# Two attention stages of a two-block transformer on one core: pairs of heads in steps with dense blocks between, and the softmax sum from a column of ones

## The chip, the cores and the metric

The kernel runs on one core of a Trainium2 chip. The metric is the device time of one execution in microseconds (us), as the median of several runs.

## What is computed

A block of 256 tokens by 1024 features runs through two models of two layers each: first gated linear attention with dense and expert feed-forward layers, then a second block whose layers are feed-forward, a mixer, an attention to a memory, and feed-forward, each with a residual and a layer norm. All of it is in fp32. The change touches the two mixers of the second block (stages `ab` and `mc`) and where the memory's keys and values are computed.

```
# ab: 8 heads of global attention and 8 heads in a window with a sink, 64 wide, 2 key heads each
s = q @ k.T * 64 ** -0.5;  p = softmax(s);  out_a = p @ v
s = where(|i - j| <= 128, s, -inf);  m = max(s.max(-1), sink)
p = exp(s - m);  p = p / (p.sum(-1) + exp(sink - m));  out_b = p @ v
y = concat(out_a, out_b) @ w_out
# mc: 16 heads of neighbourhood attention on a grid of 4 rows of 64, with a position bias
p = softmax(q @ k.T * 64 ** -0.5 + bias);  y = (p @ v) @ w_out
# memory attention, 4 heads of 256, behind each mixer
k, v = split(mem @ w_kv);  y = (softmax(q @ k.T / 16) @ v) @ w_o
```

## The kernel before

Weights are read from memory as tiles of 128 x 1024 (`split_weight`, L190): SP issues the load into `raw`, ScalarE rounds it to `whi` (L195), VectorE makes the rest `wlo` (L197). There are 7 buffers for `raw`, 9 for `whi` and 8 for `wlo`. Activations are kept as a high and a low part too (`xT`, `oT`), and a dense product is three matmuls per 128 rows of the contraction: high by high, low by high, high by low (`mm3`, L205, L207 to L209). `project` (L365) makes one or two blocks of 512 output columns of both halves `t` of the tokens, eight contraction steps each, so 24 matmuls of 512 columns for a block and half, and calls an epilogue. `out_ln` (L376) does the output projection over eight steps `k`, the residual, the layer norm and the transposition into `c.xT`.

The program is unrolled. A scheduler that knows what each instruction needs places the instructions of each engine in an order of its own, with the order of the text as priority. So work from further on in the text can stand between the pieces of a stage: the output projection of step `k` needs only the result of pair `k`.

In `mixer_ab` (L937) queries and keys of the first kind, values, and queries of the second kind come from three projected blocks (L1028, L1029). Then eight pairs of heads follow (`attend`, L1018). `mixer_c` (L1040) projects six blocks (L1097 to L1099), then has eight pairs (L1082). A pair (`pair_attention`, L920) does this:

- for each of its two heads: scores with the head's 64 features as contraction (L927), one accumulator bank for both halves of the tokens; then `soft_rows` (L870): the largest value of each row (L880 with a bias or a window, L888 without), exponentials on ScalarE with the sum of the row as a second output (L893), its reciprocal (L899), and a multiply of the probabilities by it (L901); then `rows_T` (L905): four transposes on TensorE (L911) and a copy out of PSUM, on ScalarE for the first head (L914) and VectorE for the second (L916).
- values (L932): the weights are the 64 columns of `v`, 256 columns of transposed probabilities move, the two heads write the two halves of the partitions. The result is already transposed and is split into `oT` (L285, L286), which is the same tile as `c.xT`.

The keys and values of the memory are made in eight blocks (`MemBlock`, L247): two tiles of the memory and four of weights are loaded, and two halves of dense work follow, each 24 matmuls of 512 columns or 48 of 256, each ending in a copy and a store to memory (L276, L277). `FILL` (L1153) says how many blocks go into which stage; the rest go to the start of the memory attention (L1113). Before, ab takes none and mc takes one. So mem0 has one and mem1 three.

Of the kernel before, what the change touches and what calls it, by code (L numbers as in the profile page):

```python
# [246 lines left out]
class MemBlock:  # L247
# [11 lines left out]

    def compute(self):  # L260
        c, nc = self.c, self.c.nc
        for half in range(2):
            ps = c.acc.tile([P, 512], F32, name="acc")
            if self.which == 0:
                for f in (2 * half, 2 * half + 1):
                    out = ps[:, 256 * (f % 2):256 * (f % 2) + 256]
                    for k in range(8):
                        wh, wl = self.us[k // 2]
                        sl = slice(512 * (k % 2) + P * f, 512 * (k % 2) + P * f + P)
                        mm3(c, out, wh[:, sl], wl[:, sl], *self.at(k, slice(0, 256)), k == 0, k == 7)  # L270
                o = 1024 * self.blk + 512 * half
            else:
                accumulate_k4(c, ps, lambda k: self.at(k, slice(half * P, half * P + P)), self.us)
                o = 1024 * half + 512 * self.blk
            s = c.tmp.tile([P, 512], F32, name="silu")
            nc.scalar.copy(s, ps)  # L276
            nc.sync.dma_start(c.kv[self.l][self.which][:, o:o + 512], s)  # L277
# [83 lines left out]
def tp_tile(c):  # L361
    return c.tp.tile([P, 512], F32, name="tp")

# [506 lines left out]
def soft_rows(c, ap, ps, mode, extra=None):  # L870
# [3 lines left out]
    sm = c.small.tile([P, 2], F32, name="ssm")  # L874
    p = ap.tile([P, 2, 256], F32, name="p", bufs=4)
    scale = [1.0, 1.0]
    if mode in ("bias", "window"):
# [8 lines left out]
        src = p  # L886
    else:
        nc.vector.tensor_reduce(nm, src, axis=AX.X, op=OP.max, negate=True)  # L888
        if extra is not None:
            nc.vector.tensor_mul(nm, nm, extra)  # L890
            scale = [extra[:, t:t + 1] for t in range(2)]
    for t in range(2):
        nc.scalar.activation(p[:, t], src[:, t], AF.Exp, bias=nm[:, t:t + 1], scale=scale[t],  # L893
                             accum_out=sm[:, t:t + 1])
    if mode == "window":
        es = c.small.tile([P, 2], F32, name="ses")
        nc.scalar.activation(es, nm, AF.Exp, bias=sink)
        nc.vector.tensor_add(sm, sm, es)
# [21 lines left out]
def pair_attention(c, ap, q, k, mode, extra, vsel, oT, k_out):  # L920
    nc = c.nc
    pT = []
    for a in range(2):
        r = slice(64 * a, 64 * a + 64)
        ps = acc_tile(c)
        for t in range(2):
            nc.tensor.matmul(ps[:, 256 * t:256 * t + 256], q[r, t * P:t * P + P], k[r], start=True, stop=True)  # L927
        pT.append(rows_T(c, ap, soft_rows(c, ap, ps, mode, extra(a)), a))
    po = tp_tile(c)
    for kb in range(2):  # L930
        for a in range(2):
            nc.tensor.matmul(po[64 * a:64 * a + 64, 0:256], vsel(a, kb), pT[a][:, kb], start=kb == 0, stop=kb == 1)  # L932
    split(c, po[:, 0:256], oT[0][:, k_out].rearrange("p t s -> p (t s)"),
          oT[1][:, k_out].rearrange("p t s -> p (t s)"))


def mixer_ab(c, X, xT, ln_idx):  # L937
    nc, A = c.nc, c.A
    with c.tc.tile_pool(name="ab", bufs=1) as ap:
        rope = ap.tile([P, 3, 2, 2, 64], F32, name="rope")  # L940
# [9 lines left out]
        v = ap.tile([P, 2, 256], F32, name="v")  # L950
# [30 lines left out]
        def k_epi(t, ps):  # L981
# [12 lines left out]
            nc.scalar.copy(v[:, t], ps[:, 256:])  # L994
# [16 lines left out]

        def epi0(t, pss):
            k_epi(t, pss[0])
            q_epi(t, pss[1], 0)

        oT = c.xT

        def attend(kind):  # L1018
            for hp in range(4):
                kv = hp // 2  # L1020
                pair_attention(
                    c, ap, qT[:, kind, hp], kT[:, kind, kv], "window" if kind else "plain",
                    (lambda a: ([win[:, 0], win[:, 1]], sink[:, 2 * hp + a:2 * hp + a + 1])) if kind else
                    (lambda a: rsq[:, :, 2 * hp + a]),
                    lambda a, kb: v[:, kb, 128 * kind + 64 * kv:128 * kind + 64 * kv + 64],
                    oT, 4 * kind + hp)
# [13 lines left out]
def mixer_c(c, X, xT, ln_idx):  # L1040
    nc, A = c.nc, c.A
    with c.tc.tile_pool(name="mc", bufs=1) as ap:
        nav = ap.tile([P, 64], F32, name="nav")
        nc.sync.dma_start(nav, A["nav"])
        rp = A["c_rpb"]
        v = ap.tile([P, 2, D], F32, name="v")
# [30 lines left out]
        def v_epi(t, ps, i):  # L1077
            nc.scalar.copy(v[:, t, 512 * i:512 * i + 512], ps)

        oT = c.xT  # L1080

        def attend(i):  # L1082
            for hq in range(4):
                hp = 4 * i + hq
                b = tb[hp // 2]
                if hp % 2 == 0 and hp > 0 and hp < 6:
                    tb.append(bias_tile(hp // 2 + 1))
# [13 lines left out]
        for b in extra:  # L1101
            b.load()
# [119 lines left out]
```

## Time and profile before

| | us |
|---|---|
| median of 3 runs | 2685.03 |
| lowest, highest | 2681.85, 2686.33 |
| profiled execution | 2683.43 |
| its span, first to last instruction | 2681.6 |
| TensorE busy (share of the span) | 2620.2 (98%) |
| VectorE busy | 1912.0 (71%) |
| ScalarE busy | 1492.6 (56%) |
| stage ab, attention alone | 1710 to 1766 of the span |
| stage mc, attention alone | 2302 to 2361 of the span |

The page of the profile gives for each engine its busy time, for forty slices of the span the busy tenths and the granted TensorE clock, and the costliest groups of instructions by line. Views of the trace give the same for any stretch, the waits of an engine with what ended them, and the instructions in order of time. A matmul's duration in these rows includes what it spends in the pipeline, so the distance from one start to the next says what it costs. One fp32 matmul shows as two records, one fp32 transpose as one.

### The profile page before, as it was taken

The page shows a single profiled execution, that of the slowest core. Times are in us where ns is not written, and L with a number is a line of the kernel's source. Part 1 is how long each engine was busy: PE and PEld are TensorE (multiplying, and loading weights), DVE is VectorE, ACT ScalarE, POOL GpSimd, SP SyncE. Part 2 cuts the span into 40 slices and gives each one's busy share as a digit, 9 for nine tenths or more (in the row PEclk, how much of TensorE's full clock was granted, in tenths as well). Part 3 has the DMA queues.
Part 4 walks back from the last instruction along what each step waited for, and adds up shares of the span by engine and source line. Part 5 has one row for each costly group of instructions (what it writes and reads, how often), then busy time and mean ns, then how long its engine had stood idle before and what let it go on. Part 6 is the DMA issues. An engine that isn't in the chain of part 4 may idle for free. (4 is left out here: it accounts for less than half of the span.)

```text
span 2681.6 us, 34175 instructions
## 1 busy us (share of the span) xinstructions
PE 2620.2 (98%) x12066; PEld 2103.9 (78%) x12066; DVE 1912.0 (71%) x2374; ACT 1492.6 (56%) x1844; POOL 46.9 (2%) x55
## 2 busy tenths in 40 slices
PE   8999999999999999999998999999999999999998
PEld 6888778877777877787776888678888888688887
DVE  6754668888888888888888555777546556575664
ACT  5444437677677677677666444544444444444452
POOL 1000000000000000000000000100000000000000
PEclk9999999999999999999999999899999999899999
DMA  7555537999999999999999654444555556445552
GB/s 291 174 184 177 205 118 281 340 354 341 340 346 344 347 338 353 347 338 338 361 335 339 220 188 157 168 159 163 183 194 204 188 194 194 131 173 220 204 199 91
DMA packets 193980, 658.64 MB, mean 246 GB/s; under 512 B 33094, under 2 KB 33288, under 8 KB 193288
## 3 DMA queue, kind: packets, MB, share of 16 engines
q1 hardware_dynamic: 193800, 656.37, 69.2%
q8 instruction: 96, 1.57, 0.2%
q14 instruction: 84, 0.69, 0.1%
HBM read 651.05 MB, written 5.24 MB: 245 GB/s over the span
## 5 line engine op out<-in xcount | busy, mean ns | idle before, releaser
L197 DVE TENSOR_TENSOR wlo<-raw,whi 128x1024 fp32r<-128x1024 f32 x1193 | 1407.3, 1219 | 244.7 <-ACT whi L195 114.3
L195 ACT CAST whi<-raw 128x1024 fp32r<-128x1024 f32 x1193 | 1194.0, 1051 | 373.6 <-PE acc L209 293.7
L207 PE MATMUL acc<-whi,xh 128*128 128x512 f32 x1376 | 546.0, 397 | 6.3 <-ACT whi L195 6.1
L209 PE MATMUL acc<-whi,xl 128*128 128x512 f32 x1376 | 539.4, 392 | 0.0
L208 PE MATMUL acc<-wlo,xh 128*128 128x512 f32 x1376 | 538.4, 391 | 0.1
L208 PE MATMUL acc<-wlo,xgh 128*128 128x512 f32 x896 | 356.6, 398 | 5.3 <-DVE wlo L197 5.3
L207 PE MATMUL acc<-whi,xgh 128*128 128x512 f32 x896 | 350.2, 391 | 1.8 <-ACT whi L195 1.8
L209 PE MATMUL acc<-whi,xgl 128*128 128x512 f32 x896 | 349.8, 390 | 0.0
L207 PEld LDWEIGHTS acc<-whi,xh 128*128 128x128 f32 x1376 | 259.2, 188 | 58.3 <-ACT whi L195 6.3
L209 PEld LDWEIGHTS acc<-whi,xl 128*128 128x128 f32 x1376 | 258.7, 188 | 55.4 <-issue 1.7
L208 PEld LDWEIGHTS acc<-wlo,xh 128*128 128x128 f32 x1376 | 259.3, 188 | 53.5 <-DVE wlo L197 1.6
L208 PEld LDWEIGHTS acc<-wlo,xgh 128*128 128x128 f32 x896 | 168.0, 188 | 63.1 <-DVE wlo L197 27.7
L207 PEld LDWEIGHTS acc<-whi,xgh 128*128 128x128 f32 x896 | 168.2, 188 | 40.8 <-ACT whi L195 4.8
L209 PEld LDWEIGHTS acc<-whi,xgl 128*128 128x128 f32 x896 | 168.3, 188 | 32.6
L208 PE MATMUL tp<-wlo,hTh 128*128 128x512 f32 x448 | 179.4, 400 | 7.1 <-DVE wlo L197 6.9
L209 PE MATMUL tp<-whi,hTl 128*128 128x512 f32 x448 | 177.6, 396 | 0.0
L207 PE MATMUL acc<-whi,hh 128*128 128x512 f32 x440 | 172.5, 392 | 0.0
L209 PE MATMUL acc<-whi,hl 128*128 128x512 f32 x440 | 171.3, 389 | 0.0
L208 PE MATMUL acc<-wlo,hh 128*128 128x512 f32 x440 | 171.3, 389 | 0.0
L207 PE MATMUL tp<-whi,hTh 128*128 128x512 f32 x448 | 153.3, 393 | 5.1 <-ACT whi L195 5.1
L285 ACT CAST xh<-tp 128x512 fp32r<-128x512 f32 (+1 forms) x68 | 36.1, 536 | 207.4 <-PE tp L294 158.2
L286 DVE TENSOR_TENSOR hl<-tp,hh 128x512 fp32r<-128x512 f32 (+1 forms) x60 | 38.8, 647 | 136.9 <-ACT hh L285 135.5
(241 smaller groups left out, 2423.8 us busy)
## 6 DMA issues: line engine op xcount, KB each, us to landing
raw<-moe_dram SPq DMA_DIRECT2D x672, 512.0 KB, 5.4
raw<-f_dram SPq DMA_DIRECT2D x330, 512.0 KB, 4.9
raw<-h_in_dram SPq DMA_DIRECT2D x40, 512.0 KB, 5.4
raw<-m_kv_dram SPq DMA_DIRECT2D x32, 512.0 KB, 5.0
raw<-c_in_dram SPq DMA_DIRECT2D x24, 512.0 KB, 5.2
raw<-h_out_dram SPq DMA_DIRECT2D x16, 512.0 KB, 4.5
raw<-memT_dram SPq DMA_DIRECT2D x16, 512.0 KB, 4.7
raw<-m_q_dram SPq DMA_DIRECT2D x16, 512.0 KB, 5.3
```

The source lines that it names most:

```text
L195: nc.scalar.copy(hi, raw)
L197: nc.vector.tensor_sub(lo, raw, hi.bitcast(F32))
L207: mm(ps, xh, wh, start=start, stop=False)
L208: mm(ps, xh, wl, start=False, stop=False)
L209: mm(ps, xl, wh, start=False, stop=stop)
L285: c.nc.scalar.copy(dh, ps)
L286: c.nc.vector.tensor_sub(dl, ps, dh.bitcast(F32))
```

## The change

Pairs become objects with four steps (`Pair`): `scores`, `turn` (transposes), `values`, `finish`. `attend` runs them overlapped: in step `i` first the dense fillers of that step, then `finish` of pair `i-1`, `turn` of pair `i`, `scores` of pair `i+1`, `values` of pair `i`. The fillers are the projections that only later pairs need (`late_steps`, one half of the tokens each) and the halves of the memory blocks (`MemBlock.steps`). In ab one filler goes with each of the eight pairs: two of the projection of the second kind's queries, six of three memory blocks. In mc ten: two, two, one, one for the second half's queries, keys and values, and one for each of the last four pairs, from two memory blocks. `FILL` changes from (2, (), 1, 0, 1) to (2, (), 1, 3, 2); mem0 and mem1 have none left.

The probabilities are no longer normalised. `v` has a 65th column of ones for each head (a `memset` on POOL); the values' product is turned round, so that transposed probabilities are the weights and the 65 columns move. The last column is the row sum. A reciprocal and one multiply out of PSUM normalise the 64 columns of both heads and halves; two transposes bring the result into the form of `oT`. `oT` is now a tile of its own in both stages. The filler tile `pad` shrinks from 48 to 32 columns. `soft_rows` stays as it was for the memory attention.

```diff
 class MemBlock:
+    def steps(self):
+        def first():
+            self.load()
+            self.half(0)
+
+        return [first, lambda: self.half(1)]
...
+def late_steps(c, xT, w, u0, epi):
+    us = []
+
+    def step(t):
+        if t == 0:
+            us.extend(units(c, w, u0, 2))
+        ps = acc_tile(c)
+        accumulate_k4(c, ps, tok(xT, t), us)
+        epi(t, ps)
+
+    return [lambda t=t: step(t) for t in range(2)]
...
-def pair_attention(c, ap, q, k, mode, extra, vsel, oT, k_out):
+class Pair:
+    def scores(self):
...
+            ex = self.extra(a)
+            p, src, nm, scale = row_max(c, self.ap, ps, self.mode, ex)
+            for t in range(2):
+                nc.scalar.activation(p[:, t], src[:, t], AF.Exp, bias=nm[:, t:t + 1], scale=scale[t])
+            if self.mode == "window":
+                self.es = self.es or c.small.tile([P, 2, 2], F32, name="ses")
+                nc.scalar.activation(self.es[:, :, a], nm, AF.Exp, bias=ex[1])
+            self.p.append(p)
+
+    def turn(self):
+        self.pT = [rows_T(self.c, self.ap, p, a) for a, p in enumerate(self.p)]
+
+    def values(self):
+        c, nc = self.c, self.c.nc
+        po = tp_tile(c)
+        pv = po[:, 0:260].rearrange("p (t a d) -> p t a d", t=2, a=2)
+        for a in range(2):
+            for t in range(2):
+                for kb in range(2):
+                    nc.tensor.matmul(pv[:, t, a, :], self.pT[a][:, kb, t * P:t * P + P], self.vsel(a, kb),
+                                     start=kb == 0, stop=kb == 1)
+        rc = c.small.tile([P, 2, 2], F32, name="src")
+        if self.es is None:
+            nc.vector.reciprocal(rc, pv[:, :, :, 64])
+        else:
+            nc.vector.tensor_add(rc, self.es, pv[:, :, :, 64])
+            nc.vector.reciprocal(rc, rc)
+        self.o = self.ap.tile([P, 2, 2, 64], F32, name="o", bufs=2)
+        nc.vector.tensor_mul(self.o, pv[:, :, :, 0:64], rc[:, :, :, None].to_broadcast([P, 2, 2, 64]))
+
+    def finish(self):
+        c = self.c
+        pt = tp_tile(c)
         for t in range(2):
-            nc.tensor.matmul(ps[:, 256 * t:256 * t + 256], q[r, t * P:t * P + P], k[r], start=True, stop=True)
-        pT.append(rows_T(c, ap, soft_rows(c, ap, ps, mode, extra(a)), a))
-    po = tp_tile(c)
-    for kb in range(2):
-        for a in range(2):
-            nc.tensor.matmul(po[64 * a:64 * a + 64, 0:256], vsel(a, kb), pT[a][:, kb], start=kb == 0, stop=kb == 1)
-    split(c, po[:, 0:256], oT[0][:, k_out].rearrange("p t s -> p (t s)"),
-          oT[1][:, k_out].rearrange("p t s -> p (t s)"))
+            c.nc.tensor.transpose(pt[:, t * P:t * P + P], self.o[:, t].rearrange("p a d -> p (a d)"), c.ident)
+        split(c, pt[:, 0:256], self.oT[0][:, self.k_out].rearrange("p t s -> p (t s)"),
+              self.oT[1][:, self.k_out].rearrange("p t s -> p (t s)"))
+
+
+def attend(pair, n, fillers):
+    cur, last = pair(0), None
+    cur.scores()
+    for i in range(n):
+        for f in fillers.get(i, ()):
+            f()
+        if last is not None:
+            last.finish()
+        cur.turn()
+        nxt = None
+        if i + 1 < n:
+            nxt = pair(i + 1)
+            nxt.scores()
+        cur.values()
+        cur, last = nxt, cur
+    last.finish()
...
 def mixer_ab(c, X, xT, ln_idx):
+        oT = pair_tile(ap, "oT")
...
-        oT = c.xT
...
         project(c, A["ab_in"], 0, 2, xT, epi0)
-        project(c, A["ab_in"], 4, 1, xT, lambda t, pss: q_epi(t, pss[0], 1))
-        extra = take(c, c.F[3])
-        for b in extra:
-            b.load()
-        attend(0)
-        attend(1)
-        for b in extra:
-            b.compute()
+        steps = late_steps(c, xT, A["ab_in"], 4, lambda t, ps: q_epi(t, ps, 1))
+        for b in take(c, c.F[3]):
+            steps += b.steps()
+        attend(pair, 8, {i: [f] for i, f in enumerate(steps)})
...
 def mixer_c(c, X, xT, ln_idx):
+        oT = pair_tile(ap, "oT")
...
         project(c, W, 0, 2, xT, lambda t, pss: (q_epi(t, pss[0], 0), k_epi(t, pss[1], 0)))
-        project(c, W, 4, 2, xT, lambda t, pss: (v_epi(t, pss[0], 0), q_epi(t, pss[1], 1)))
-        project(c, W, 8, 2, xT, lambda t, pss: (k_epi(t, pss[0], 1), v_epi(t, pss[1], 1)))
-        extra = take(c, c.F[4])
-        for b in extra:
-            b.load()
-        attend(0)
-        attend(1)
-        for b in extra:
-            b.compute()
+        project(c, W, 4, 1, xT, lambda t, pss: v_epi(t, pss[0], 0))
+        steps = []
+        for n, f in enumerate((q_epi, k_epi, v_epi)):
+            steps += late_steps(c, xT, W, 6 + 2 * n, lambda t, ps, f=f: f(t, ps, 1))
+        for b in take(c, c.F[4]):
+            steps += b.steps()
+        plan = {0: steps[0:2], 1: steps[2:4], 2: steps[4:5], 3: steps[5:6]}
+        for i, f in enumerate(steps[6:]):
+            plan.setdefault(4 + i % 4, []).append(f)
+        attend(pair, 8, plan)
...
-FILL = (2, (), 1, 0, 1)
+FILL = (2, (), 1, 3, 2)
```

## Rows read from the trace of the kernel before

**Rows 1.** The page, forty slices of the span: granted TensorE clock in tenths.

```profile
PEclk9999999999999999999999999899999999899999
```

**Rows 2.** Windows over the attentions: length, busy us (instructions) per engine, clock, DMA share, GB/s.

```profile
1710.25:1765.60 55.35, 52.19 (x223) 28.40 (x221) 34.33 (x133) 29.04 (x91) 0.00 (x0) 0.88 0.09 29
2302.10:2361.00 58.90, 55.50 (x232) 33.72 (x232) 35.44 (x146) 26.92 (x84) 0.00 (x0) 0.74 0.28 63
```

**Rows 3.** Windows cut where the granted clock changes, ab first, then mc.

```profile
1716.60:1730.20 13.60, 12.82 (x32) 6.31 (x32) 6.32 (x22) 5.74 (x19) 0.00 (x0) 0.50 0.00 0
1730.20:1765.60 35.40, 35.29 (x170) 19.55 (x169) 23.40 (x102) 19.91 (x67) 0.00 (x0) 1.00 0.00 1
2307.10:2317.30 10.20, 10.18 (x29) 5.62 (x29) 4.94 (x25) 3.01 (x12) 0.00 (x0) 0.50 0.58 91
2317.30:2331.00 13.70, 12.07 (x59) 6.64 (x60) 10.24 (x40) 6.64 (x21) 0.00 (x0) 1.00 0.41 59
2331.00:2351.50 20.50, 19.87 (x62) 11.85 (x60) 11.89 (x53) 8.15 (x28) 0.00 (x0) 0.50 0.00 0
2351.50:2361.00 9.50, 9.50 (x64) 6.65 (x62) 5.05 (x18) 4.14 (x13) 0.00 (x0) 1.00 0.01 2
```

**Rows 4.** Waits of TensorE in the two attentions: us in total, times, longest.

```profile
PE acc L927 <- ACT p L893: 2.5, 1, 2.5
...
PE tp L911 <- DVE p L901: 1.8, 2, 1.1
```

**Rows 5.** Timeline of TensorE's matmuls in ab at full clock: start, length, group.

```profile
1753.77 0.65 PE L932 MATMUL tp<-pT,v 128*64 128x256 f32 x2
1754.35 0.50 PE L207 MATMUL acc<-whi,xh 128*128 128x512 f32 x1
1754.69 0.39 PE L208 MATMUL acc<-wlo,xh 128*128 128x512 f32 x1
1755.01 1.08 PE L932 MATMUL tp<-pT,v 128*64 128x256 f32 x6
1756.02 0.50 PE L209 MATMUL acc<-whi,xl 128*128 128x512 f32 x1
...
1756.58 0.60 PE L911 MATMUL tp<-cst,p 128*128 128x128 f32 x4
1756.94 0.48 PE L208 MATMUL acc<-wlo,xh 128*128 128x512 f32 x1
...
1757.96 0.39 PE L209 MATMUL acc<-whi,xl 128*128 128x512 f32 x1
1758.18 0.39 PE L207 MATMUL acc<-whi,xh 128*128 128x512 f32 x1
```

**Rows 6.** Timeline of TensorE in the first stage, fp32 products with few moving columns.

```profile
30.89 0.95 PE L466 MATMUL tp<-cst,m 128*128 128x2 f32 x8
31.70 0.49 PE L208 MATMUL acc<-wlo,xh 128*128 128x512 f32 x1
...
65.80 1.13 PE L580 MATMUL tp<-vg,wsm 128*128 128x128 f32 x8 [1.20 <-DVE vg L576]
66.69 0.48 PE L207 MATMUL acc<-whi,xh 128*128 128x512 f32 x1
```

**Rows 7.** Groups by line, ab's attention, then its full-clock stretch: busy us, mean ns, idle.

```profile
L901 DVE TENSOR_SCALAR p<-p,ssm 128x256 f32<-128x256 f32 x32 | 9.9, 347 | 0.0
...
L911 PE MATMUL tp<-cst,p 128*128 128x128 f32 x53 | 10.1, 290 | 0.1
L207 PE MATMUL acc<-whi,xh 128*128 128x512 f32 x9 | 3.9, 428 | 0.0
```

**Rows 8.** The page, costliest groups: the VectorE half of splitting a weight tile.

```profile
L197 DVE TENSOR_TENSOR wlo<-raw,whi 128x1024 fp32r<-128x1024 f32 x1193 | 1407.3, 1219 | 244.7 <-ACT whi L195 114.3
```

**Rows 9.** Windows, columns as in rows 2: ab's start, and mc's end with mem1.

```profile
1673.90:1684.90 11.00, 11.00 (x53) 8.94 (x52) 11.00 (x17) 4.91 (x7) 4.41 (x7) 1.00 0.86 299
2361.00:2470.00 109.00, 108.94 (x577) 92.76 (x576) 72.80 (x91) 56.49 (x79) 1.83 (x2) 1.00 0.67 241
```

More of the change, by code (lines that the diff above doesn't have):

```diff
@@ L258, in at, with half @@
         return [x[:, o + sl.start:o + sl.stop] for x in self.m[k // 4]]
+    def half(self, half):
+        c, nc = self.c, self.c.nc
+        ps = c.acc.tile([P, 512], F32, name="acc")
+        if self.which == 0:
+            for f in (2 * half, 2 * half + 1):
+                out = ps[:, 256 * (f % 2):256 * (f % 2) + 256]
+                for k in range(8):
+                    wh, wl = self.us[k // 2]
+                    sl = slice(512 * (k % 2) + P * f, 512 * (k % 2) + P * f + P)
+                    mm3(c, out, wh[:, sl], wl[:, sl], *self.at(k, slice(0, 256)), k == 0, k == 7)
+            o = 1024 * self.blk + 512 * half
+        else:
+            accumulate_k4(c, ps, lambda k: self.at(k, slice(half * P, half * P + P)), self.us)
+            o = 1024 * half + 512 * self.blk
+        s = c.tmp.tile([P, 512], F32, name="silu")
+        nc.scalar.copy(s, ps)
+        nc.sync.dma_start(c.kv[self.l][self.which][:, o:o + 512], s)
     def compute(self):
-        c, nc = self.c, self.c.nc
         for half in range(2):
[L263 to L277, printed above, removed]
+            self.half(half)
+    def steps(self):
[3 more added lines that the diff above has]
+        return [first, lambda: self.half(1)]
 def take(c, n):
@@ L867, in crowded, with row_max @@
             step()
[L870 removed]
+def row_max(c, ap, ps, mode, extra):
     nc = c.nc
@@ L885, in soft_rows @@
             nc.vector.tensor_scalar(nm, nm, sink, -1.0, op0=OP.max, op1=OP.mult)
[L886 to L891, printed above, removed]
-    for t in range(2):
[L893 to L898, printed above, removed]
+        return p, p, nm, [1.0, 1.0]
+    nc.vector.tensor_reduce(nm, src, axis=AX.X, op=OP.max, negate=True)
+    if extra is None:
+        return p, src, nm, [1.0, 1.0]
+    nc.vector.tensor_mul(nm, nm, extra)
+    return p, src, nm, [extra[:, t:t + 1] for t in range(2)]
+def soft_rows(c, ap, ps):
+    nc = c.nc
+    sm = c.small.tile([P, 2], F32, name="ssm")
+    p, src, nm, _ = row_max(c, ap, ps, "plain", None)
+    for t in range(2):
+        nc.scalar.activation(p[:, t], src[:, t], AF.Exp, bias=nm[:, t:t + 1], accum_out=sm[:, t:t + 1])
     nc.vector.reciprocal(sm, sm)
@@ L949, in mixer_ab @@
         qT = ap.tile([P, 2, 4, 256], F32, name="qT")
-        v = ap.tile([P, 2, 256], F32, name="v")
+        v = ap.tile([P, 2, 4, 65], F32, name="v")
+        nc.gpsimd.memset(v[:, :, :, 64:65], 1.0)
         tab = ap.tile([P, 2, 2, 2, 64], F32, name="tab")
@@ L1010, in q_epi, with pair @@
             nc.scalar.copy(qT[:, kind, :, t * P:t * P + P], pt.rearrange("p (b s) -> p b s", b=4))
+        def pair(i):
+            kind, hp = i // 4, i % 4
+            kv = hp // 2
+            return Pair(
+                c, ap, qT[:, kind, hp], kT[:, kind, kv], "window" if kind else "plain",
+                (lambda a: ([win[:, 0], win[:, 1]], sink[:, 2 * hp + a:2 * hp + a + 1])) if kind else
+                (lambda a: rsq[:, :, 2 * hp + a]),
+                lambda a, kb: v[:, kb, 2 * kind + kv], oT, i)
         def epi0(t, pss):
@@ L1045, in mixer_c @@
         rp = A["c_rpb"]
-        v = ap.tile([P, 2, D], F32, name="v")
+        v = ap.tile([P, 2, 16, 65], F32, name="v")
+        nc.gpsimd.memset(v[:, :, :, 64:65], 1.0)
         qT = [ap.tile([P, 4, 256], F32, name=f"qT{i}") for i in range(2)]
@@ L1077, in v_epi @@
         def v_epi(t, ps, i):
[L1078 to L1087, printed above, removed]
-                pair_attention(
-                    c, ap, qT[i][:, hq], kT[i][:, hq], "bias",
-                    lambda a: ([b[:, 2 * (hp % 2) + a, 2 * t:2 * t + 4, :].rearrange("p u c -> p (u c)")[:, ::-1]
-                                for t in range(2)], None),
-                    lambda a, kb: v[:, kb, 128 * hp + 64 * a:128 * hp + 64 * a + 64],
-                    oT, hp)
+            nc.scalar.copy(v[:, t, 8 * i:8 * i + 8, 0:64], ps.rearrange("p (h d) -> p h d", d=64))
@@ L1170, in body @@
         xT = c.xT = pair_tile(c.xtp, "x")
-        nc.gpsimd.memset(pad.tile([P, 48], F32, name="pad"), 0.0)
+        nc.gpsimd.memset(pad.tile([P, 32], F32, name="pad"), 0.0)
         c.early = []
```

43 lines of the change are left out of this document (25 added, 18 removed).

## Prediction

> **What bounds the kernel now.** I went from the whole to the stage. The page's line of the granted TensorE clock [rows 1] is full in nearly every fortieth of the span; its two dips, the 26th and the 35th slice (67 us each), are the two stages that the diff touches. TensorE is busy almost throughout, so in this kernel a microsecond counts when TensorE stands still, runs at half clock, or gets more work. The other engines matter only through these three.
>
> Next the windows over the two attentions [rows 2]: 55.35 us in ab and 58.90 us in mc, with mean clocks 0.88 and 0.74. Busy time there is 52.19 and 55.50 us, but busy says little, since a matmul at half clock counts as busy for twice as long. Cutting the windows where the clock changes shows it [rows 3]. In ab 13.6 us are at 0.50 (1.2 GHz) and 35.4 us at 1.00 (2.4 GHz). In mc 10.2 and 20.5 us are at 0.50, 13.7 and 9.5 us at 1.00. Before the fall in ab TensorE stood still for 2.5 us on the first exponentials (L893), and one of its waits in mc is on the normalisation L901, which this change removes [rows 4]. The full-clock stretch of ab matters for later: the same attention, with only some 25 dense matmuls strewn into it (9 of them the L207 of a triple), kept 2.4 GHz for 35 us [rows 3, 7]. DMA moved next to nothing there and VectorE was busy 34.33 of 55.35 us, so neither bounds [rows 2].
>
> **Step 1, half clock.** The dense work that used to come before and after the attention (late projections, memory blocks) now stands between the pairs: 8 half-blocks of 24 matmuls with 512 columns in ab (or 48 with 256), 10 in mc, one or two per pair. TensorE then has something to run while a softmax is under way. I price it by records per us. In ab 32 records took 13.6 us at half clock, and 170 took 35.4 us at full clock, 0.208 us each; 32 x 0.208 = 6.7, so 6.9 us go. In mc 29 + 62 = 91 records took 30.7 us, and 59 + 64 = 123 took 23.2 us at full clock, 0.189 each; 91 x 0.189 = 17.2, so 13.5 us go. **Together -20.4 us.** Most of the expected gain is here.
>
> **Step 2, standing still.** Idle TensorE is 55.35 - 52.19 = 3.2 us in ab and 58.90 - 55.50 = 3.4 us in mc [rows 2]; of that 0.8 and 0.6 us lie in the half-clock stretches and are already counted [rows 3]. The rest, 2.4 + 2.8, should be covered by the dense halves: **-5.2 us**. If the cover is not ready in time this term is zero.
>
> **Step 3, values.** Before, a pair's value product is 8 records with 256 moving columns on two column halves of the array. In two runs of the timeline they take 1754.35 - 1753.77 = 0.58 and 1756.02 - 1755.01 = 1.01 us, 1.59 together [rows 5]. After, it is 16 records: the probabilities are the 128x128 weights, 65 columns move (64 values and the column of ones), and each fp32 product is two records, as now. No row has 65 columns, so I bound it by rows with the same weights: 2 columns, eight in 31.70 - 30.89 = 0.81 us; 128 columns, eight in 66.69 - 65.80 = 0.89 us [rows 6]. Both ends are close, so the weight load sets it: 16 records take 1.62 to 1.78 us. I take the upper. The result lies by query rows now, so `finish` adds two transposes; four cost 1756.94 - 1756.58 = 0.36 [rows 5], two 0.18, plus some 0.07 to get in and out. Sum per pair 1.78 + 0.25 - 1.59 = 0.44 us (0.21 at the low end), sixteen pairs: **+7.0 us** (+3.4). This is real work on the busiest engine, and the price of the new form.
>
> **Step 4, dense matmuls in a row.** A dense 512-column matmul in a block starts 0.22 us after the one before (1757.96 to 1758.18), a lone one between attention pieces 0.34 (1754.35 to 1754.69) [rows 5]. In ab some dozen of the 25 in the full-clock stretch pay that 0.1 us; in mc I assume the same. Blocks of 24 don't: **-2 us**, with 0 and -3 as ends, because whoever orders the queue may still cut the blocks.
>
> **Step 5, VectorE and ScalarE.** Gone are the normalisation L901, 9.9 us in one attention [rows 7], and the read of the row sum behind each exponential on ScalarE. Added per pair are a small reciprocal, one multiply of 256 columns out of PSUM and, in window mode, one small add; the nearest row for the multiply is L901's 347 ns, its upper bound twice that, at most 16 x 1 us with the rest. TensorE doesn't feel either: **0 us**, hidden under some 10 us per pair of TensorE work. Without the cover the longer end of a pair (multiply, transposes, split) would cost about 1.5 us once per stage, behind the last pair.
>
> **Step 6, what moves.** The memory blocks leave mem0 (one) and mem1 (three) for ab (three) and mc (two, one of them there before). Their TensorE time is the same in either place, since mem1 with the end of mc is busy 108.94 of 109.00 us [rows 9]: 0 us. Without them the projection behind `out_ln` must cover the layer norm alone. The start of ab has just that form: 11.00 of 11.00 us busy, at full clock, with VectorE busy for all 11.00 too [rows 9], so it holds but has no slack. Each block brings six weight tiles, at 1219 ns of VectorE each [rows 8], 7.3 us for two pair steps of some 10 us; VectorE was 60% busy and loses L901, so it fits. On SP each `kv` store waits for its half-block's copy, and the weight loads queued behind it wait too; then `split_weight` is late for the next half-block. As DMA share was 0.09 in ab [rows 2], I cost it at nothing, with the ends in the next step. The `memset` of the ones on POOL and the smaller pad cost nothing. `oT` in its own tile lets late projections still read `xT`; by itself it gives no time.
>
> **Step 7, new waits.** Six tiles for a half-block that is due after some 5 us of attention may come late, the half-clock stretches may not all go, and the last pair's chain stands bare. From zero to 8 us (half of the 16 pairs late by 1 us, the size of one tile); I take **+3**.
>
> **Sum.** -20.4 - 5.2 + 7.0 - 2 + 3 = -17.6 us. The profiled execution took 2683.43 us (span 2681.6); so 2665.8. The median of the three runs, 2685.03, lies 1.6 above it, so I forecast 2667.
>
> **A rule against it.** In ab's full-clock stretch 53 transposes are among the 170 records, and the clock is 1.00 throughout [rows 3, 7]. The Trainium skill ("TensorE: Matmul & The Clock Gate", Part 4: PE-mode transpose) states that transposes don't count as activity for the clock in the way that matmuls do. The change adds transposes and takes moving columns away, so by that rule the clock would fall between the blocks (rival C). The trace doesn't bear it out so far.
>
> **Rivals.** *A, the forecast*, 0.63: -17.6. Its own range runs from all ends favourable (+3.4, -3, 0: -25) to all unfavourable (+7, 0, +8: -10.6): 2660 to 2674.
> *B, half of it stays*, 0.17: blocks are drawn ahead of the pairs that should be covered, and half of the half-clock time remains: +10.2, 2677. Still faster.
> *D, the blocks wait for weights*, 0.10: six tiles take 7.3 us on VectorE, the attention piece beside them has about 3.3 us of its own VectorE work ((34.33 - 9.9) / 8 = 3.05, and some of late epilogues), against 5 us of TensorE attention; 3 us late at each of five blocks, or about 15 us in all: 2682, no measurable change. For it: VectorE without slack in the 11.00 us window [rows 9]. Against: those are 10 us steps, not 5.
> *C, the clock falls between the dense blocks*, 0.10, the other side: the attention pieces are now narrower (65 columns) and follow each other in 5 us pieces, 16 x 5 = 80 us of them (records of step 3, plus scores and transposes at 0.2 us). Each us at 1.2 GHz costs half a us. From 47 us of half clock on it is slower by 5.4 us; at 55 us it is 2667 + 27 = 2694. Against it stand the 35.4 us at 1.00 with far less dense work [rows 3].
> That the order isn't as the text has it, is in B.
>
> **How the numbers follow.** A difference of 0.2% (5.4 us) is about what a measurement of this kernel can tell from no change. A and B are faster, 0.80; D is the same, 0.10; C is slower, 0.10. The range reaches from 2655 (A's best end with a little more of the standing still) to 2684, which takes in B and D and leaves C out and a little below.
>
> **What would show it.** Step 1: mean clock of ab and mc attention near 1.00, no stretch at 0.50 over 7 us. Step 2: no wait of TensorE over 1 us there. Step 3: the value records some 0.11 us apart, 16 to a pair. Step 4: dense matmuls 0.23 us apart in runs of twenty or more. Step 6: mem0 and mem1 each shorter by their blocks' time, busy as before. Wrong if TensorE waits for ScalarE's or VectorE's weight tiles inside the attention (D), or if half clock appears between blocks (C).

## The result and the profile after

The changed kernel takes 2656.42 us (median of four runs, 2655.05 to 2656.5) against 2685.42 for the kernel before in the same comparison: a ratio of 0.9893, interval [0.9876, 0.991]. That is 29.0 us less. The prediction had 2667 in a range of 2655 to 2684: the direction and the wide range hold, the latter by 1.4 us at its low end. The forecast's own range ended at 2660: its sum had left out a term of 10 us, the scores, and had a smaller one with the wrong sign.

The page after, to be held against [rows 1]: its first line, TensorE's busy time, and the clock in forty slices.

```profile
span 2654.6 us, 34354 instructions
...
PE 2596.9 (98%) x12226; PEld 2110.3 (79%) x12226; DVE 1899.9 (72%) x2306; ACT 1483.8 (56%) x1780; POOL 46.8 (2%) x57
...
PEclk9999999999999999999999999999999999999999
```

The two dips of the kernel before are gone. The windows over the two attentions (ab from the first scores to the last pair, then mc; columns as in [rows 2]) say it more sharply:

```profile
1701.20:1781.20 80.00, 78.73 (x543) 68.08 (x544) 52.85 (x120) 45.52 (x82) 1.63 (x1) 1.00 0.45 149
2281.20:2370.70 89.50, 88.87 (x503) 72.44 (x502) 57.70 (x136) 51.83 (x83) 0.00 (x0) 1.00 0.61 185
```

They are longer than the 55.35 and 58.90 us of [rows 2] because dense work has moved in, and the clock is 1.00 (2.4 GHz) in both, where it was 0.88 and 0.74. TensorE stands still for 1.27 and 0.63 us, where it was 3.2 and 3.4. All its waits in ab, then in mc (us in total, times, longest), against [rows 4]:

```profile
PE acc L955 <- ACT kT L1077: 0.8, 1, 0.8
PE acc L955 <- DVE ry L1056: 0.5, 1, 0.5
PE tp L975 <- ACT pT L936: 0.3, 2, 0.2
```

```profile
PE tp L1141 <- ACT qs L1136: 0.3, 1, 0.3
PE tp L1141 <- DVE qs L1138: 0.2, 1, 0.2
```

None is on an exponential, a normalisation or a weight tile.

Where the time goes by stage can be read from POOL. The last layer-norm instruction of each stage is the second of its pair at L328 (`lrs`). In the timeline of POOL (start, length, group) the last one ahead of ab, of ab, of mem0, ahead of mc, of mc and of mem1:

```profile
1681.67 0.92 POOL L328 TENSOR_TENSOR lrs<-lrs,cst 128x1 f32<-128x1 f32 x1 [5.05 <-DVE lrs L327]
...
1813.68 0.93 POOL L328 TENSOR_TENSOR lrs<-lrs,cst 128x1 f32<-128x1 f32 x1 [14.31 <-DVE lrs L327]
...
1877.82 0.92 POOL L328 TENSOR_TENSOR lrs<-lrs,cst 128x1 f32<-128x1 f32 x1 [14.32 <-DVE lrs L327]
```

```profile
2251.23 0.92 POOL L328 TENSOR_TENSOR lrs<-lrs,cst 128x1 f32<-128x1 f32 x1 [5.02 <-DVE lrs L327]
...
2402.92 0.92 POOL L328 TENSOR_TENSOR lrs<-lrs,cst 128x1 f32<-128x1 f32 x1 [14.32 <-DVE lrs L327]
...
2467.03 0.92 POOL L328 TENSOR_TENSOR lrs<-lrs,cst 128x1 f32<-128x1 f32 x1 [14.32 <-DVE lrs L327]
```

So ab takes 1813.68 - 1681.67 = 132.0 us, mem0 64.1, mc 151.7 and mem1 64.1, together 411.9. The same marks in the trace of before give 109.3, 75.0, 159.4 and 97.3, together 441.0. The difference is 29.1 us. The two profiled executions differ by 27.0 (spans of 2681.6 and 2654.6), because everything outside these four stages takes 2240.6 us in the one and 2242.7 in the other; of the ten kernels in the table below seven lie from the one to the other, these two among them, so the gain is in the four stages. mem0 and mem1 are shorter by 10.9 and 33.2 us, one and three blocks of 10.9 to 11.1; ab takes in three blocks for 22.7 more, and mc takes in one block and is still 7.7 shorter.

One group of the timeline of TensorE explains a part of this that the prediction had left out. A pair in ab, after:

```profile
1731.53 0.38 PE L990 MATMUL tp<-cst,o 128*128 128x128 f32 x2
1731.75 1.04 PE L933 MATMUL tp<-cst,p 128*128 128x128 f32 x8
1732.71 1.14 PE L955 MATMUL acc<-kT,qT 64*128 64x256 f32 x8
1733.78 2.00 PE L975 MATMUL tp<-v,pT 128*128 128x65 f32 x16
1735.59 0.48 PE L207 MATMUL acc<-whi 128*128 128x512 f32 x1
...
1740.93 0.39 PE L209 MATMUL acc<-whi,wlo 128*128 128x512 f32 x1
1741.16 0.38 PE L990 MATMUL tp<-cst,o 128*128 128x128 f32 x2
```

The second line of score matmuls, L955: eight records, four for each head, from 1732.71 to the next start at 1733.78, which is 1.07 us. Experiment 5 shows what four of them cost alone.

### The profile page after: what moved, and what is told of

Same layout as the page of the kernel before. It is cut to its first block, busy times and chain, and to the rows that moved or that the text cites. A ratio compares the mean times of both kernels' runs of the same rounds, so it can differ in the third digit from the quotient of the medians.

```text
span 2654.6 us, 34354 instructions
## 1 busy us (share of the span) xinstructions
PE 2596.9 (98%) x12226; PEld 2110.3 (79%) x12226; DVE 1899.9 (72%) x2306; ACT 1483.8 (56%) x1780; POOL 46.8 (2%) x57
## 5 line engine op out<-in xcount | busy, mean ns | idle before, releaser
L207 PE MATMUL acc<-whi,xh 128*128 128x512 f32 x1312 | 522.0, 398 | 6.6 <-ACT whi L195 6.3
L209 PE MATMUL acc<-whi,xl 128*128 128x512 f32 x1312 | 514.9, 393 | 0.0
L208 PE MATMUL acc<-wlo,xh 128*128 128x512 f32 x1312 | 514.1, 392 | 0.0
L207 PEld LDWEIGHTS acc<-whi,xh 128*128 128x128 f32 x1312 | 247.5, 189 | 56.5 <-ACT whi L195 6.3
L209 PEld LDWEIGHTS acc<-whi,xl 128*128 128x128 f32 x1312 | 247.0, 188 | 52.0 <-issue 0.5
L208 PEld LDWEIGHTS acc<-wlo,xh 128*128 128x128 f32 x1312 | 247.5, 189 | 50.1 <-DVE wlo L197 0.8
L295 ACT CAST xh<-tp 128x512 fp32r<-128x512 f32 x52 | 30.2, 588 | 172.9 <-PE tp L304 159.2
```

The costliest lines, as they stand in the source:

```text
L207: mm(ps, xh, wh, start=start, stop=False)
L208: mm(ps, xh, wl, start=False, stop=False)
L209: mm(ps, xl, wh, start=False, stop=stop)
L295: c.nc.scalar.copy(dh, ps)
```

## The experiments

Every kernel here computes the whole result. The experiments carry the numbers of their kernels. The theories that the expectations name are these.
- Theory 1: dense blocks between the pairs give the gain, since TensorE no longer falls to half clock. Rival 2: the new pair form (steps, column of ones) gives it, wherever the dense work stands.
- Rival 3 is about the scores: it says that it is worth nothing whether the two heads' scores stand next to each other on TensorE.
- Theory 4: the overlapped steps keep TensorE fed. Theory 5: the column of ones does, by taking the normalisation out of the chain from scores to transposes.
- Theories 6 to 8 are told with their runs.

All times by run, with the ratio to the kernel before in the same comparison and its interval; then the stages by the marks above, and the time at half clock inside the attentions of ab and mc. The kernel before was measured anew with each group of experiments, at 2682.57 to 2685.42 us, so a difference of 2 or 3 us between two rows of different groups tells nothing.

| kernel | us | ratio | ab | mem0 | mc | mem1 | half clock, ab / mc |
|---|---|---|---|---|---|---|---|
| before | 2685.42 | 1 | 109.3 | 75.0 | 159.4 | 97.3 | 13.7 / 30.7 |
| after | 2656.42 | 0.9893 [0.9876, 0.991] | 132.0 | 64.1 | 151.7 | 64.1 | 0 / 0 |
| e1 old places of dense work | 2670.75 | 0.9954 [0.9938, 0.9969] | 108.3 | 75.0 | 145.7 | 97.3 | 13.7 / 0 |
| e2 old values, dense blocks | 2649.66 | 0.9874 [0.9859, 0.9889] | 126.3 | 64.1 | 146.7 | 64.1 | 0 / 0 |
| e3 no memory blocks moved | 2661.41 | 0.9918 [0.9903, 0.9934] | 102.5 | 75.0 | 142.2 | 97.4 | 0 / 0 |
| e5 heads' scores apart | 2666.48 | 0.9936 [0.9922, 0.995] | 137.4 | 64.1 | 157.4 | 64.1 | 0 / 0 |
| e7 steps alone | 2699.04 | 1.0059 [1.0042, 1.0076] | 113.0 | 75.0 | 167.0 | 97.3 | 23.9 / 47.8 |
| e8 dense blocks alone | 2657.64 | 0.9906 [0.9889, 0.9922] | 131.9 | 64.1 | 153.8 | 64.1 | 0 / 0 |
| e9 old places, ones, and normalised | 2711.4 | 1.0105 [1.0088, 1.0122] | 114.9 | 75.1 | 174.6 | 97.3 | 23.9 / 58.0 |
| e10 old places, old order, ones | 2671.84 | 0.9958 [0.9941, 0.9974] | 108.7 | 75.0 | 146.1 | 97.4 | 13.7 / 0 |

**1. The dense work back at its old places.** The new steps and the column of ones stay; the late projections and memory blocks stand before and after the attention again, and `FILL` is the old one.

```diff
-        steps = late_steps(c, xT, A["ab_in"], 4, lambda t, ps: q_epi(t, ps, 1))
-        for b in take(c, c.F[3]):
-            steps += b.steps()
-        attend(pair, 8, {i: [f] for i, f in enumerate(steps)})
+        project(c, A["ab_in"], 4, 1, xT, lambda t, pss: q_epi(t, pss[0], 1))
+        extra = take(c, c.F[3])
+        for b in extra:
+            b.load()
+        attend(pair, 8, {})
+        for b in extra:
+            b.compute()
...
-FILL = (2, (), 1, 3, 2)
+FILL = (2, (), 1, 0, 1)
```

> The new pairs (column of ones, overlapped steps, own oT) with the dense work where it stood before: projections ahead of the attention, memory blocks as before. Theory 1 (the dense blocks between the pairs give the gain: they keep 2.4 GHz, fill the waits, and leave both heads' scores side by side): the half clock and the waits return and the new value form costs its 7 us, so 2680 to 2692 us, with stretches at clock 0.50 in both attentions. Rival 2 (the new form of the pair gives it: no normalisation on the way from exponential to transposes, steps overlapped): within 6 us of the changed kernel, 2652 to 2662 us, no half clock.

Measured: 2670.75 us, between the two ranges. The windows show why neither number fits. ab, cut where its clock changes, then the whole attention of mc:

```profile
1711.80:1717.60 5.80, 3.86 (x22) 2.67 (x21) 4.45 (x9) 3.07 (x4) 0.00 (x0) 1.00 0.75 258
1717.60:1731.30 13.70, 13.12 (x46) 9.06 (x48) 5.21 (x13) 7.06 (x15) 0.00 (x0) 0.50 0.00 1
1731.30:1766.80 35.50, 34.55 (x240) 28.23 (x240) 20.81 (x76) 16.70 (x42) 0.00 (x0) 1.00 0.00 1
2302.40:2347.00 44.60, 42.63 (x306) 35.29 (x306) 29.29 (x114) 23.94 (x51) 0.00 (x0) 1.00 0.35 79
```

ab falls for 13.7 us as before, mc not at all. So for the full clock the dense blocks are needed in ab, while something in the pair's new form is enough in mc. Theory 1 holds for one stage of two.

**2. The value product as it was, with the steps and the dense blocks of the change.** Probabilities are normalised again ahead of the transposes.

```diff
+            nc.vector.reciprocal(sm, sm)
+            for t in range(2):
+                nc.vector.tensor_scalar(p[:, t], p[:, t], sm[:, t:t + 1], None, op0=OP.mult)
...
-                    nc.tensor.matmul(pv[:, t, a, :], self.pT[a][:, kb, t * P:t * P + P], self.vsel(a, kb),
-                                     start=kb == 0, stop=kb == 1)
...
+                nc.tensor.matmul(self.po[64 * a:64 * a + 64, 0:256], self.vsel(a, kb)[:, 0:64], self.pT[a][:, kb],
+                                 start=kb == 0, stop=kb == 1)
...
-            c.nc.tensor.transpose(pt[:, t * P:t * P + P], self.o[:, t].rearrange("p a d -> p (a d)"), c.ident)
```

> The dense blocks stay between the pairs; normalisation, row sums and the value product go back to the old form (two heads on two column halves, 256 moving columns, result already transposed). Theory 1: 16 records at 0.111 us and two transposes, 2.0 us a pair, go; eight records take their place, 1.1 us if they stand together (two at a time) and 1.59 if they are cut as before; so 7 to 14 us faster than the changed kernel, 2642 to 2650 us, with the clock at 1.00. Rival 2 (the new pair form gives the gain): VectorE gets 1.4 us of normalisation per pair back on the chain, 2670 to 2685 us.

Measured: 2649.66 us, in theory 1's range, 6.8 less than the change as a whole, and the fastest kernel here. The column of ones costs time where dense blocks stand between the pairs. The stages say 10.7 us (126.3 + 146.7 against 132.0 + 151.7); 3.9 of that are given back where the edit touches nothing. Outside the four stages this kernel takes 2246.4 us, and e7 and e9 take 2247.2, against at most 2242.7 in the other seven. The three have in common that the tile `src` is gone while `pad` keeps its 32 columns (before and e8 have no `src` either, but a `pad` of 48); whether the place of the tiles in memory is the cause wasn't tried. The same pair as above, in this kernel's timeline:

```profile
1732.63 1.03 PE L933 MATMUL tp<-cst,p 128*128 128x128 f32 x8
1733.59 1.14 PE L955 MATMUL acc<-kT,qT 64*128 64x256 f32 x8
1734.66 1.08 PE L979 MATMUL tp<-pT,v 128*64 128x256 f32 x8
1735.68 0.50 PE L207 MATMUL acc<-whi 128*128 128x512 f32 x1
```

The old value product takes 1735.68 - 1734.66 = 1.02 us in one piece, against 1.81 for the new one (1733.78 to 1735.59 above) and 0.22 for its two transposes (1731.53 to 1731.75).

**3. The memory blocks back, the late projections still between the pairs.** This is one line.

```diff
-FILL = (2, (), 1, 3, 2)
+FILL = (2, (), 1, 0, 1)
```

> Late projections still stand between the pairs, but the memory blocks go where they were (none in ab, one in mc). Six of eight pairs of ab and two of mc have no filler of their own. Theory 1: part of the half clock returns in ab, less in mc, and scores are cut apart again in ab: 5 to 14 us slower than the changed kernel, 2661 to 2670 us. Rival 2: no change, 2653 to 2660 us.

Measured: 2661.41 us, 5.0 more than after, at the low end of theory 1's range. Of the two reasons given for it one fails: no half clock came back, so the late projections alone keep 2.4 GHz in ab and mc. The other, scores cut apart in ab, is what its timeline shows:

```profile
1723.84 1.04 PE L933 MATMUL tp<-cst,p 128*128 128x128 f32 x8
1724.80 1.13 PE L955 MATMUL acc<-kT,qT 64*128 64x256 f32 x4
1725.86 2.00 PE L975 MATMUL tp<-v,pT 128*128 128x65 f32 x16
1727.79 1.13 PE L955 MATMUL acc<-kT,qT 64*128 64x256 f32 x6
```

Here one head's four score records take 1.06 us (1724.80 to 1725.86). The distances from each of the 64 score records of ab to the next start add up to 15.2 us (waits included), against 10.5 after: 4.7 of the 5.0.

**5. The second head's scores kept apart from the first's.** Everything else is the change.

```diff
-            nxt.scores()
+            nxt.scores((0,))
         cur.values()
+        if nxt is not None:
+            nxt.scores((1,))
```

> The changed kernel with the second head's scores issued behind the value product of the pair before; in some 12 of 16 pairs the two heads' scores no longer stand side by side on TensorE. Theory 1 with its new term (in the changed kernel eight score records of two heads take 1.07 us, because the heads' 64 rows run at the same time; alone a head's four take 1.06): 12 pairs lose 0.8 to 1.1 us each, 9 to 13 us slower than the changed kernel, 2665 to 2670 us. Rival 3 (side by side or not, the scores are hidden or cost the same): within 3 us of the changed kernel.

Measured: 2666.48 us, 10.1 more than after and in theory 1's range; 5.4 more in ab, 5.7 in mc. The pair of above in its timeline:

```profile
1732.64 1.13 PE L956 MATMUL acc<-kT,qT 64*128 64x256 f32 x4
1733.70 2.00 PE L976 MATMUL tp<-v,pT 128*128 128x65 f32 x16
1735.63 1.13 PE L956 MATMUL acc<-kT,qT 64*128 64x256 f32 x4
1736.69 0.50 PE L207 MATMUL acc<-whi 128*128 128x512 f32 x1
```

Four records 1.06 us, and four more another 1.06: twice the 1.07 of the eight together. That is no fixed price of a group of score records: two alone take 0.63 us (in e3 and e8). One head's features lie on partitions 0 to 63 and the other's on 64 to 127, and four records of the second head add nothing to the four of the first, so the two heads run at the same time if nothing stands between them in TensorE's queue. The Trainium skill ("TensorE: Matmul & The Clock Gate", Part 3: Packing small matmuls — row/col tiling) says that matmuls with a contraction under 128 on distinct row groups run concurrently; this trace agrees, with 1.07 against 2.12 us.

**7. The steps alone.** Old places of the dense work as in e1, old values and normalisation as in e2; what stays of the change are the overlapped steps and `oT` in its own tile.

```diff
-            if self.mode == "window":
-                self.es = self.es or c.small.tile([P, 2, 2], F32, name="ses")
...
+            nc.vector.reciprocal(sm, sm)
+            for t in range(2):
+                nc.vector.tensor_scalar(p[:, t], p[:, t], sm[:, t:t + 1], None, op0=OP.mult)
...
-        attend(pair, 8, plan)
+        project(c, W, 4, 2, xT, lambda t, pss: (v_epi(t, pss[0], 0), q_epi(t, pss[1], 1)))
+        project(c, W, 8, 2, xT, lambda t, pss: (k_epi(t, pss[0], 1), v_epi(t, pss[1], 1)))
...
+        attend(pair, 8, {})
```

> Dense work where it stood before, and the old form of values, sums and normalisation; what is left of the change is the overlapped steps (next pair's scores ahead of this pair's values) and oT in its own tile. It tells apart what gave the 13 us of the run with the old staging, whose mc attention had no half clock. Theory 4 (the overlap keeps TensorE fed): about 7 us less than that run, since the old values are cheaper: 2660 to 2668 us, no half clock in mc. Theory 5 (the column of ones does it, because no normalisation stands between exponential and transposes): the half clock of mc returns, 2678 to 2690 us.

Measured: 2699.04 us, 16.1 more than the kernel before (11.3 of it in the four stages) and beyond both expectations, on the side of theory 5. Two of the three windows at half clock, the one of ab and the first of mc's two:

```profile
1720.40:1744.30 23.90, 21.69 (x55) 10.07 (x55) 8.95 (x31) 9.78 (x30) 0.00 (x0) 0.50 0.02 8
...
2317.70:2348.40 30.70, 30.70 (x83) 15.56 (x83) 13.46 (x54) 9.51 (x31) 0.00 (x0) 0.50 0.24 52
```

Overlapping the pairs doesn't keep TensorE fed when the normalisation is on the way and no dense work stands by.

**8. The dense blocks alone.** The pair is that of the kernel before (its order, normalisation and values); the dense halves stand between the pairs. The cut is against the kernel before.

```diff
         def attend(kind):
             for hp in range(4):
+                for f in plan.get(4 * kind + hp, ()):
+                    f()
                 kv = hp // 2
                 pair_attention(
...
-FILL = (2, (), 1, 0, 1)
+FILL = (2, (), 1, 3, 2)
```

> The old attention of a pair as it stood (normalised probabilities, old values, no overlapped steps), with only the dense blocks put between the pairs and oT in its own tile for them. Theory 1 (dense blocks between pairs are what the gain needs): like the run with the old values in the new steps, 2647 to 2656 us, clock 1.00 in both attentions. Theory 4 (overlap is needed too): the softmax of a pair isn't covered where its dense block runs out, 2658 to 2672 us, with waits of TensorE on L901 or L893.

Measured: 2657.64 us, between the two ranges, and not to be told from the change as a whole (1.2 us). No half clock. Against e2 it is 8.0 us slower, and its timeline shows that the scheduler cuts the work otherwise:

```profile
1733.23 0.49 PE L934 MATMUL tp<-cst,p 128*128 128x128 f32 x3
1733.47 0.47 PE L208 MATMUL acc<-wlo,whi 128*128 128x512 f32 x1
1733.88 0.65 PE L955 MATMUL tp<-pT,v 128*64 128x256 f32 x2
1734.45 0.50 PE L209 MATMUL acc<-whi,wlo 128*128 128x512 f32 x1
...
1735.83 1.08 PE L955 MATMUL tp<-pT,v 128*64 128x256 f32 x6
1736.84 0.50 PE L208 MATMUL acc<-wlo,whi 128*128 128x512 f32 x1
```

Its values take 0.57 + 1.01 = 1.58 us here, because a dense matmul cuts them into two and six; in e2's steps they stand whole at 1.02. Counted over the four stages as in the next section, e8 needs 304.0 us for dense matmuls, 25.3 for values and 23.0 for scores, where e2 needs 296.8, 20.6 and 19.5; only the transposes of probabilities are cheaper, 12.7 against 14.6.

**9 and 10. What in the pair's form keeps mc at full clock.** e1 and e7 differ in two things: the normalisation ahead of the transposes, and the value product with its records. e9 puts only the normalisation, with the row sum and reciprocal that it needs, back into e1 (what comes out of the new value product is copied, not multiplied). e10 takes e1 and puts the pairs in the old order, one after the other and head by head, without overlap. Theory 6 is the wait through the normalisation, theory 7 the extra records, theory 8 that mc needs both the steps and the short chain.

```diff
+            nc.vector.reciprocal(sm, sm)
+            for t in range(2):
+                nc.vector.tensor_scalar(p[:, t], p[:, t], sm[:, t:t + 1], None, op0=OP.mult)
...
-        nc.vector.tensor_mul(self.o, pv[:, :, :, 0:64], rc[:, :, :, None].to_broadcast([P, 2, 2, 64]))
+        nc.vector.tensor_copy(self.o, pv[:, :, :, 0:64])
```

> The pair steps with the dense work at its old places, the value product in its new form with the column of ones (16 records of 65 columns and two transposes to a pair), but with the probabilities normalised on VectorE ahead of their transposes, as before; what comes out of the value product is copied instead of multiplied. It tells apart what keeps mc at full clock without dense blocks between the pairs. Theory 6 (the wait: a pair's transposes stand on TensorE behind exponential, sum, reciprocal and normalisation, and it is this longer chain that lets the clock fall): half clock comes back in mc, 30 to 50 us of it, and the time is 2685 to 2705. Theory 7 (the records: the new value product and its transposes give TensorE more to do in every pair, and that keeps the clock): no half clock in mc as in the kernel with the old staging, 2670 to 2676, the longer chain showing only as some waits.

```diff
-        if last is not None:
-            last.finish()
-        cur.turn()
-        nxt = None
-        if i + 1 < n:
-            nxt = pair(i + 1)
-            nxt.scores()
+        cur = pair(i)
+        cur.scores()
         cur.values()
-        cur, last = nxt, cur
+        cur.finish()
```

> The column of ones alone: the new value product, without normalisation on the way, but the pairs one after the other as before (scores, transposes, values and finish of a pair, head by head, before the next pair), the dense work at its old places, oT in its own tile. Theory 6 (the wait through the normalisation): mc keeps 2.4 GHz or falls for 10 us at most, and ab falls for about 14 us as in the kernel before; scores of the two heads stand apart again, so about 2672 to 2682. Theory 8 (both are needed in mc, the overlapped steps and the short chain): half clock in mc of 20 to 30 us as before, 2685 to 2700, since the value product is dearer by 7.

Measured: e9 2711.4 us, 40.6 more than e1 (35.5 of it in the four stages) and above the top of theory 6's range; e10 2671.84, just under the low end of theory 6's and not to be told from e1 (1.1 us). In e9 the whole of mc from its first pair on is at half clock, and in e10 none of it. Window of e9, then of e10:

```profile
2320.90:2378.90 58.00, 55.72 (x203) 43.90 (x202) 28.00 (x112) 17.31 (x58) 0.00 (x0) 0.50 0.13 28
```

```profile
2302.80:2347.00 44.20, 42.07 (x300) 34.23 (x298) 29.18 (x112) 24.15 (x51) 0.00 (x0) 1.00 0.37 82
```

Theory 7 falls: e9 has the new records and more of them than before, and has the most half clock of all. Theory 8 falls: e10 has no steps and keeps its clock. That `oT` has its own tile is not it either, since e7 has that too and falls. How mc begins in e9's timeline, right ahead of the fall at 2320.9:

```profile
2313.78 3.88 PE L955 MATMUL acc<-kT,qT 64*128 64x256 f32 x24
2318.71 0.81 PE L933 MATMUL tp<-cst,p 128*128 128x128 f32 x4 [1.04 <-DVE p L968]
2319.45 1.13 PE L955 MATMUL acc<-kT,qT 64*128 64x256 f32 x4
```

And in e1's, where no fall follows:

```profile
2302.41 3.13 PE L955 MATMUL acc<-kT,qT 64*128 64x256 f32 x20
2305.98 0.33 PE L933 MATMUL tp<-cst,p 128*128 128x128 f32 x1 [0.44 <-ACT p L959]
```

TensorE's first stop in mc is 1.04 us on the normalisation L968 in e9 and 0.44 us on the exponential L959 in e1. In the kernel before, the fall in mc comes behind a stop on the normalisation too ([rows 4], the longest 1.1 us). This is what TensorE did before the clock fell; that the stop itself is the cause is read from it, not tried separately. That the normalisation on the way brings the half clock, where no dense work stands by, is shown by e9 against e1.

## Why the prediction was right, and where its steps were wrong

To hold each step against the traces I add up the distances from one start on TensorE to the next over ab, mem0, mc and mem1, by what the first of the two does; waits are counted apart. What starts at half clock is counted at half of its distance, and the other half is put under half clock. (Eight value records take 0.91 us at full clock, 1726.87 to 1727.78 in after, and 1.74 at half, 2321.09 to 2322.83 in e9, so a half is right within a few per cent. Sums in the table are of unrounded figures.)

| us over the four stages | before | after | change | forecast |
|---|---|---|---|---|
| half clock (step 1) | 21.5 | 0 | -21.5 | -20.4 |
| standing still (steps 2 and 7) | 6.4 | 2.1 | -4.4 | -5.2 + 3 |
| values, with the transposes of results (step 3) | 25.0 | 31.8 | +6.8 | +7.0 |
| dense matmuls (steps 4 and 6) | 293.6 | 296.4 | +2.7 | -2 |
| scores | 29.8 | 19.8 | -10.0 | none |
| transposes of probabilities | 17.5 | 14.6 | -3.0 | none |
| everything else | 47.0 | 47.4 | +0.4 | none |
| together | 440.9 | 412.1 | -28.8 | -17.6 |

**Steps 1 and 2 (half clock, standing still): right.** Each sign that was to show them is there: clock 1.00 in both windows and no wait over 0.8 us. Of the standing still in the two attentions 1.9 us remain, mostly at ab's start on the rotated queries and keys. **Step 7 (+3)** wasn't needed.

**The cause given in step 1 was incomplete.** It put all the half clock down to dense work missing between the pairs. e8 shows that this work alone removes all of it, so for this change the step gives the right number. But in mc it is not the only thing that does: without any dense block the column of ones, alone, removes mc's 30.7 us (e10). In these runs the half clock of mc came only where two things met, a pair without dense work beside it and a normalisation ahead of the transposes. In ab, where the first wait is on the exponentials (e1: 1.9 us in two waits on L959, and the clock falls), the shorter chain leaves 13.7 us as before, and only the dense work removes them.

**Step 3 (values): right for this change.** The new form takes 0.113 us a record against the 0.111 taken. The old one, put at 1.59 us a product from one that a dense matmul had cut in two, comes to 25.0 / 16 = 1.56 in the trace of before. What the step doesn't price is the old form in the new order: there it comes to 20.6 us over the sixteen pairs (e2), 1.02 where it stands whole, so in the changed kernel the column of ones costs 11.2.

**Step 4 (dense matmuls, -2): wrong in sign.** The 24 from 1735.59 to 1741.16 stand in a row, at 0.232 each, as the step said. But the four stages together pay 2.7 us more for dense matmuls than before, 4.7 away from the term. A dense matmul with another kind of work right ahead of it still has a longer distance to the next (1735.59 to 1735.91, 0.32), and at full clock there are 72 of them where there were 60: the blocks brought breaks of their own. In e8 there are 117, and the dense matmuls take 10.4 more than before.

**Step 5 (VectorE and ScalarE, 0) was right with the cover.** With dense blocks e2 has the normalisation back and TensorE has no wait on it. Without cover the step priced only what the change adds behind the multiply, 1.5 us once per stage, and put what it takes off the chain between scores and transposes at nothing. That chain is worth more: e9 against e1 costs 35.5 us in the four stages. e9 is at half clock for 68.2 us more in the two attentions (23.9 + 58.0 against 13.7), which is some 34 of them.

**Step 6 (moved blocks, 0) was right.** mem0 and mem1 are shorter by just one and three blocks, TensorE is busy 69.22 of 69.30 us in the window from mc's end into mem1, and no wait on a weight tile stands in the attentions.

**The missing term: the scores.** This is the step that failed: the prediction took a pair's scores over unchanged, at nothing. It saw `scores` become one step for both heads and didn't ask what the change does to the order on TensorE. Before, the two heads' scores mostly stood apart; after, nearly all stand as eight neighbours. That is -10.0 us, from 29.8 to 19.8, and e5, which sets them apart again, is back at 30.1 and 10.1 us slower. The one step for both heads doesn't bring this by itself: the steps without dense blocks are at 30.1 (e7), the dense blocks without steps at 23.0 (e8), both at 19.5 (e2). The price could have been read from the trace of before. One head's four records take 1.06 us where they stand alone (1742.45 to 1743.51), while twenty of several heads at mc's start take 3.35 (0.17 each) up to the wait behind them:

```profile
1742.45 1.13 PE L927 MATMUL acc<-kT,qT 64*128 64x256 f32 x4
...
2302.64 3.35 PE L927 MATMUL acc<-kT,qT 64*128 64x256 f32 x20
2307.12 1.08 PE L911 MATMUL tp<-cst,p 128*128 128x128 f32 x4 [1.13 <-DVE p L901]
```

Without the scores the change in the four stages is -18.8 against the forecast -17.6. That this is so near is partly luck: step 4 erred by 4.7 one way, and half clock, standing still and the transposes of probabilities together by some 6 the other. That the result still lies in the wide range is luck too, since the prediction took it down to 2655 for a little more of the standing still, and not for the scores.

The rivals didn't come. Rival B (blocks drawn ahead of the pairs) and D (waits for weights) left no trace. Rival C expected the clock to fall between the blocks; the clock is 1.00 throughout, with 128 transposes of probabilities in the sixteen pairs. By the rule that spoke for it (the Trainium skill, "TensorE: Matmul & The Clock Gate", Part 4: PE-mode transpose) transposes wouldn't hold the clock. Here they stand among other matmuls, so no run separates them, and the rule is neither borne out nor refuted.

## What to carry to other kernels

In one of the two attentions half clock had two remedies, dense work between the pairs or a shorter chain from scores to transposes; in the other only the first helped. Once the first covers a stage, the second is worth nothing there and its price remains, so try each alone before both (e2, without the column of ones, is the fastest here). When steps are regrouped, price also the operations whose code doesn't change: what stands next to what on TensorE can be worth more than what was added. And a price read from one stretch holds for the order of that stretch: the cut value product priced this change well, and misses what the same product costs whole.

## What the runs showed of the hardware

- Two fp32 products with a contraction of 64, on partitions 0 to 63 and 64 to 127, run at the same time when neighbours in the queue: eight records in 1.07 us, against 1.06 for four of one alone. With 16 records of 65 columns between them nothing is shared (1.06 + 1.06).
- An fp32 record with 128 x 128 weights and 65 moving columns starts 0.113 us after the one before. That is no less than with 128 columns (0.111, from [rows 6]) and little over 2 columns (0.101), so up to 128 moving columns such a product's price hardly depends on them.
- TensorE's busy time doesn't tell its clock. e9 is at 0.50 for 58.0 us of mc with TensorE busy for 55.72 of them; e10 is at 1.00 in mc with 42.07 of 44.20.
